# A new beginning for a two-layer hybrid decoder trunk: x in four pieces on the scalar queue, six early weight chunks, the first products by high parts, idle products between the first transposes

## The chip, the cores and the metric

The kernel runs on one core of a Trainium2 chip. The time is device time of that core in microseconds for one execution of the whole program. The core has TensorE (matrix products; PE in the rows, with PEld for the loading of its stationary operand), VectorE (DVE), ScalarE (ACT), GpSimd (POOL) and SyncE (SP), which here only issues DMAs. ScalarE can issue DMAs too; its queue is a second one beside SyncE's. Each engine works through its own instructions in order and waits on semaphores for the others.

## The reference, cut to what matters

Two layers over 256 tokens of 1024 features, all in float32:

```python
def hybrid_layer(x, ...):
    h = rms_norm(x, attn_pre_gain)
    u = h @ w_in                       # 1024 x 4120
    (qa, ka, va, qb, kcb, vcb, ksb, vsb, kwb, vwb, g_nsa, g_a, g_b) = jnp.split(u, offsets, axis=-1)
    o_a = swa_sink_attention(rope(qa), rope(ka), va, attn_sinks)
    o_b = nsa_attention(...)           # compressed, selected and window branches, gated
    mixed = sigmoid(g_a) * (o_a @ w_branch_a) + sigmoid(g_b) * (o_b @ w_branch_b)
    x = x + rms_norm(mixed @ w_out, attn_post_gain)
    h = rms_norm(x, ffn_pre_gain)
    x = x + rms_norm(conv_ffn(h, ffn_w_up, ffn_conv_w, ffn_conv_b, ffn_w_down), ffn_post_gain)
    return x
```

Only the beginning of the first layer is touched: x, its norm, and the first columns of `h @ w_in`.

## The kernel before, in words

**Split products.** A float32 product is made of three products of float32r operands. Both operands are split into a high part (rounded to float32r) and a low part (what is left): high x high, high x low and low x high are added up in PSUM (`mm3`, lines 366 to 368). For a weight chunk ScalarE writes the high part (`copy`, line 114, tile `wh`) and VectorE the low part (`sub`, line 117, tile `wl`). For x the same two engines make `xh` and `xl`; both are called `x` in the rows.

**The weight stream.** `Stream` holds all weight chunks in order of use. `load` has SyncE fetch a chunk of 512 KB into one of four staging buffers `st` (line 156); a buffer comes free when the chunk's low part has been made. `high` makes the high part and returns a function that makes the low part; `make` does both. Below, W0, W1, ... are the chunks in order: the first column tile of `w_in` (512 columns) has W0 to W3, each with 256 of the 1024 rows, the second W4 to W7, the third W8 to W11. The framework's scheduler orders each engine's instructions as they were written and as operands come free; the last argument of a chunk and `W.make` set how far ahead it is made.

**DMA lanes.** Every DMA signals on one of eight semaphores in turn, and its issue waits until the DMA eight places ahead of it has landed. So at most eight are outstanding, and an issue that waited shows when an older one landed.

**The beginning.** The tokens are two tiles of 128 (t = 0, 1). x is first loaded in three DMAs: half the features of t = 0 on ScalarE's queue (line 260), the other half, and the whole of t = 1, on SyncE's (lines 263, 265), between W0, W1 and W2. `x(t,h)` below is half h of token tile t. `first_T` transposes such a half by four transposes (line 410) and VectorE multiplies it with the gain (line 412); `first_split` has ScalarE write the high part and returns the low part. The scale of the norm itself, `rstd`, is applied later, in rope. While TensorE has nothing to do, `warm(n)` gives it n idle products of 512 columns on a tile of zeros (line 1124); `WARM` says how many stand ahead of the first transposes and how many behind them. A PSUM bank of the tag `T` (two of them) takes each group of transposes.

**The order around it.** `in_tile` runs the products of one column tile: for each chunk c and token tile t six products (two of the chunk's 128-row slices, three each). `FIRST` is the order of the pairs (t, c) in the first column tile, and `HOOKS` says which steps (further transposes, chunks to be made, `rest`) are written ahead of which pair. `rest` has ScalarE square x (line 362), GpSimd make `rstd` and its scale (lines 354, 355, 496), and VectorE, ScalarE and GpSimd the rope tables (lines 328 to 349). When a tile is done, `rope` on VectorE reads its banks, `rstd` and the tables (lines 466 to 470); `stack_T` transposes its results on TensorE (line 477) some parts later. A part is one call of `go`; `later(20, ...)` is due 20 parts on.

Of the kernel before, what the change touches and what calls it, by code (L numbers as in the profile page):

```python
# [9 lines left out]
F32 = mybir.dt.float32  # L10
# [6 lines left out]
P = 128  # L17
# [35 lines left out]
DL = {'qa0': 2, 'qa1': 13, 'ka': 6, 'qb0': 8, 'qr0': 8, 'qb1': 2, 'qr1': 4, 'cb0': 1, 'cb1': 3, 'ks': 1, 'kw': 6, 'pT': (3, 3, 2), 'pv': 4, 'hT': 1, 'ge': 3, 'pj': 4, 'cT': 5, 'cv': 9, 'yT': 1, 'h0': 5, 'h1': 4, 'uf': 0, 'x0': 3, 'x1': 3}  # L53
WARM = (6, 8)
HOOKS = {0: '1C', 1: 'B2', 2: 'D', 6: '3r'}
FIRST = [(0, 0), (0, 1), (1, 0), (1, 1), (0, 2), (1, 2), (0, 3), (1, 3)]
CMPI = (0, 0, 0, 0, 4, 6, 7, 8)
# [8 lines left out]
def tile_hybrid_trunk(  # L66
# [78 lines left out]
    class Stream:  # L145
        def __init__(self):
            self.specs, self.loaded, self.made, self.used, self.front = [], {}, {}, 0, 0

        def add(self, src, a, b, tag="w", ahead=2):
# [3 lines left out]
        def load(self, i):  # L153
            src, a, b, tag, _ = self.specs[i]
            st = wp.tile([P, a, b], F32, tag="st", bufs=4, name=nm("st"))
            nc.sync.dma_start(st, src)
            self.loaded[i] = st, a, b, tag

        def make(self, i=None):
# [99 lines left out]
    nc.sync.dma_start(cst[:, 0:P], consts[:, 0:P])  # L259
    act.dma_start(halves(X[:, 0, :])[0], halves(xv[:, 0, :])[0])  # L260
    nc.sync.dma_start(grow, attn_pre_gain[0].rearrange("(k p) -> k p", p=P))
    W.load(0)
    nc.sync.dma_start(halves(X[:, 0, :])[1], halves(xv[:, 0, :])[1])
    W.load(1)
    nc.sync.dma_start(X[:, 1, :], xv[:, 1, :])
    W.load(2)
    W.load(3)
    last_sq = [None]
# [18 lines left out]
    sink = cp.tile([P, DEPTH, 8], F32, name="sink")  # L287
    nc.sync.dma_start(sink, attn_sinks.partition_broadcast(P))
    row_load(R_B1, cmp_b1.rearrange("l k h -> (l k) h"))
    row_load(R_POS, cmp_pos_emb.rearrange("l k (pr two) d -> (l k pr) (two d)", two=2))  # L290
# [130 lines left out]
    def attn_layer(l, xp, rs, gains, first):  # L421
# [3 lines left out]
        done = set()  # L425

        def in_tile(i, tag, fin, tmajor=False, hooks={}):
            c0, w = IN_TILES[i]
# [3 lines left out]
            def go(t, c):  # L432
                if c not in chs:
                    chs[c] = W.next(2, w)
                ch = chs[c]
                tk = slice(t * P, (t + 1) * P)
                for k in range(2):
                    kk = 2 * c + k
                    o, wh, wl = bk[t][:, :w], ch[0][:, k, :], ch[1][:, k, :]
                    if i == 2:  # L440

                        o = o.rearrange("p (y x d) -> p y x d", x=2, y=2)
                        wh, wl = [v.rearrange("p (x y d) -> p y x d", x=2, y=2) for v in (wh, wl)]
                    mm3(o, xh[:, kk, tk], xl[:, kk, tk], wh, wl, kk == 0, kk == 7)
# [672 lines left out]
    def start():  # L1117
# [11 lines left out]
        dve.tensor_copy(gfirst, gb[:, 0:KD])  # L1129
        low = first_split(0, 0, first_T(0, 0), xp)  # L1130
        warm(WARM[1])
        lw = W.high(0)
        low()
        lw()

        def xs(*args):
            lows = [first_split(t, h, first_T(t, h), xp) for t, h in args]
            for f in lows:
                f()

        def rest():
            for t in range(2):
                rs[t] = rstd_of(mean_sq(halves(X[:, t, :])))
            dve.tensor_scalar(nsink, sink, -1.0, None, ALU.mult)
            rope_tables()
        act_ = {"B": lambda: xs((0, 1)), "C": lambda: xs((1, 0)), "D": lambda: xs((1, 1)), "X": lambda: xs((1, 0), (1, 1)),
                "1": lambda: W.make(1), "2": lambda: W.make(2), "3": lambda: W.make(3), "r": rest, "w": lambda: warm(3)}
        return {FIRST[i]: [act_[c] for c in h] for i, h in HOOKS.items()}

# [86 lines left out]
```

## Time and profile before

| | us |
|---|---|
| median of 3 runs | 794.11 |
| lowest and highest | 791.46, 797.75 |
| the profiled execution | 794.85 |
| its span | 793.0 |
| TensorE busy in it | 765.7 |
| VectorE, ScalarE, GpSimd busy | 613.2, 495.4, 48.1 |

The span runs from the first instruction to the last; the rest of the execution's time lies around it. In the rows, times are microseconds from the span's start. A row of the timeline is an instruction, or several alike that followed each other: start, time taken, engine, line of the kernel, operation, tile written <- tiles read (buffer numbers left out), shape, and count; in brackets how long the engine had been idle before, and what ended it. A row of a DMA queue (SPq, ACTq) is the issue of a transfer, not the transfer. A product's time in a row includes its way through the array: where products follow each other, the step from start to start is what one costs.

### The profile page before, as it was taken

The page shows a single profiled execution, that of the slowest core. Times are in us where ns is not written, and L with a number is a line of the kernel's source. Part 1 is how long each engine was busy: PE and PEld are TensorE (multiplying, and loading weights), DVE is VectorE, ACT ScalarE, POOL GpSimd, SP SyncE. Part 2 cuts the span into 40 slices and gives each one's busy share as a digit, 9 for nine tenths or more (in the row PEclk, how much of TensorE's full clock was granted, in tenths as well). Part 3 has the DMA queues.
Part 4 walks back from the last instruction along what each step waited for, and adds up shares of the span by engine and source line. Part 5 has one row for each costly group of instructions (what it writes and reads, how often), then busy time and mean ns, then how long its engine had stood idle before and what let it go on. Part 6 is the DMA issues. An engine that isn't in the chain of part 4 may idle for free.

```text
span 793.0 us, 12908 instructions
## 1 busy us (share of the span) xinstructions
PE 765.7 (97%) x4745; PEld 682.0 (86%) x4745; DVE 613.2 (77%) x1168; ACT 495.4 (62%) x948; POOL 48.1 (6%) x96
## 2 busy tenths in 40 slices
PE   8999999999899999999989999999998999999996
PEld 6689888888699999999868889888877999999995
DVE  5898888676778767777788888886867877778775
ACT  4678877744666555665555879767555655556552
POOL 2300022100100000000010000230001000000000
PEclk9999999999999999999999999999999999999999
DMA  7633156456556656666435232644645666656731
GB/s 268 218 111 123 41 160 216 144 172 205 166 168 196 187 185 183 209 218 186 157 118 173 74 121 86 206 151 135 205 137 182 193 185 186 186 184 212 216 105 53
DMA packets 42202, 131.26 MB, mean 166 GB/s; under 512 B 5359, under 2 KB 5915, under 8 KB 42139
## 3 DMA queue, kind: packets, MB, share of 16 engines
q1 hardware_dynamic: 41995, 130.18, 51.4%
q8 instruction: 37, 0.61, 0.3%
q10 hardware_dynamic: 144, 0.26, 0.1%
q14 instruction: 26, 0.21, 0.1%
HBM read 129.37 MB, written 1.05 MB: 164 GB/s over the span
## 4 chain that ended last, share of the span: by engine, by line
PE 81%; DVE 7%; ACT 7%; POOL 2%; issue 2%; DMA 1%; SPq 0%; DVEq 0%; POOLq 0%; ACTq 0%
PE mm L366 6%; PE mm L367 6%; PE mm L368 6%; PE S L367 5%; PE S L368 5%; PE S L366 5%; PE T L1000 5%; PE T L999 5%; PE mm L1000 5%; PE mm L999 5%; PE T L998 5%; PE mm L998 5%; PE O L366 3%; PE O L367 3%; PE O L368 3%; DVE wl L117 2%
## 5 line engine op out<-in xcount | busy, mean ns | idle before, releaser
L117 DVE TENSOR_TENSOR wl<-st,wh 128x1024 fp32r<-128x1024 f32 (+2 forms) x226 | 268.0, 1188 | 101.1 <-ACT wh L114 99.7
L114 ACT ACTIVATE wh<-st 128x1024 fp32r<-128x1024 f32 (+2 forms) x226 | 231.8, 1029 | 170.9 <-PE O L368 40.1
L366 PE MATMUL mm<-wh,x 128*128 128x512 f32 (+2 forms) x256 | 97.3, 382 | 0.1
L367 PE MATMUL mm<-wl,x 128*128 128x512 f32 (+2 forms) x256 | 96.2, 376 | 0.0
L368 PE MATMUL mm<-wh,x 128*128 128x512 f32 (+2 forms) x256 | 95.2, 372 | 0.0
L999 PE MATMUL mm<-q,wh 128*128 128x256 f32 x320 | 90.7, 283 | 0.0
L999 PE MATMUL T<-q,wh 128*128 128x256 f32 x320 | 90.6, 283 | 0.0
L1000 PE MATMUL T<-q,wl 128*128 128x256 f32 x320 | 90.6, 283 | 0.0
L1000 PE MATMUL mm<-q,wl 128*128 128x256 f32 x320 | 90.5, 283 | 0.0
L998 PE MATMUL T<-q,wh 128*128 128x256 f32 x320 | 90.5, 283 | 0.0
L998 PE MATMUL mm<-q,wh 128*128 128x256 f32 x320 | 90.4, 283 | 0.0
L998 PEld LDWEIGHTS mm<-q,wh 128*128 128x128 f32 x320 | 61.3, 192 | 0.9
L998 PEld LDWEIGHTS T<-q,wh 128*128 128x128 f32 x320 | 61.4, 192 | 0.8
L999 PEld LDWEIGHTS mm<-q,wh 128*128 128x128 f32 x320 | 61.3, 192 | 0.8
L999 PEld LDWEIGHTS T<-q,wh 128*128 128x128 f32 x320 | 61.4, 192 | 0.7
L1000 PEld LDWEIGHTS mm<-q,wl 128*128 128x128 f32 x320 | 61.3, 192 | 0.1
L1000 PEld LDWEIGHTS T<-q,wl 128*128 128x128 f32 x320 | 61.4, 192 | 0.0
L368 PEld LDWEIGHTS mm<-wh,x 128*128 128x128 f32 x256 | 49.2, 192 | 6.3
L366 PEld LDWEIGHTS mm<-wh,x 128*128 128x128 f32 x256 | 49.2, 193 | 5.8 <-ACT k L114 0.4
L367 PEld LDWEIGHTS mm<-wl,x 128*128 128x128 f32 x256 | 49.4, 193 | 5.6 <-DVE wl L117 0.3
L607 ACT ACTIVATE k<-k,mn 128x128 f32<-128x128 f32 (+1 forms) x96 | 42.5, 446 | 8.4 <-DVE mn L604 8.4
L354 POOL TENSOR_SCALAR rstd<-s 128x1 f32<-128x1 f32 x16 | 6.1, 381 | 520.7 <-ACT k L362 520.5
(293 smaller groups left out, 1672.9 us busy)
## 6 DMA issues: line engine op xcount, KB each, us to landing
st<-in_ffn_w_up_dram SPq DMA_DIRECT2D x88, 512.0 KB, 4.3
st<-in_w_in_dram SPq DMA_DIRECT2D x48, 512.0 KB, 3.8
st<-in_ffn_w_down_dram SPq DMA_DIRECT2D x44, 512.0 KB, 4.3
st<-in_w_out_dram SPq DMA_DIRECT2D x16, 512.0 KB, 3.6
st<-in_w_in_dram SPq DMA_DIRECT2D x16, 384.0 KB, 3.1
st<-in_cmp_w_dram SPq DMA_DIRECT2D x16, 256.0 KB, 2.6
st<-in_w_branch_a_dram SPq DMA_DIRECT2D x8, 512.0 KB, 3.6
st<-in_w_branch_b_dram SPq DMA_DIRECT2D x8, 512.0 KB, 3.6
```

Of the source, the lines that this page charges most:

```text
L114: act.activation(dst, src, AF.Copy, scale=scale)
L117: dve.tensor_tensor(dst, a, b, ALU.subtract)
L354: pool.tensor_scalar(r, s2[:, 0:1], s2[:, 1:2], EPS, ALU.add, ALU.add)
L366: pe.matmul(o, xh, wh, start=first, stop=False, skip_group_check=True)
L367: pe.matmul(o, xh, wl, start=False, stop=False, skip_group_check=True)
L368: pe.matmul(o, xl, wh, start=False, stop=last, skip_group_check=True)
L607: last_exp[0] = act.activation(self.pt[:, hh, s, :], sm[:, :nk], AF.Exp, bias=self.mn[:, i:i + 1], scale=-1.0, accum_out=self.dn[:, i:i + 1])
L998: pe.matmul(o, wh[:, k, :], hh[:, k, c0:c1], start=(k == 0), stop=False, skip_group_check=True)
L999: pe.matmul(o, wh[:, k, :], hl[:, k, c0:c1], start=False, stop=False, skip_group_check=True)
L1000: pe.matmul(o, wl[:, k, :], hh[:, k, c0:c1], start=False, stop=(k == 7), skip_group_check=True)
```

## The change

x comes in four pieces of 256 KB, all issued by ScalarE, in the order x(0,0), x(1,0), x(0,1), x(1,1). SyncE loads W0 to W3 and, behind the constants, W4 to W9 too, ahead of the small row loads. W4 to W9 don't use staging buffers: they land in three large tiles (tags `sg` and `kB`), which the attention writes much later. Both token tiles' first halves are transposed ahead of the first product, with two idle products between and three behind (`WARM`). Chunks 0 and 1 go through `products`, which for chunk 0 takes high x high of both token tiles first, then the products with the weight's low part, then those with x's. The transposes of the other halves stand behind all products of chunk 0, and the steps of the old table `HOOKS` are now written out in `start`.

```diff
-WARM = (6, 8)
-HOOKS = {0: '1C', 1: 'B2', 2: 'D', 6: '3r'}
-FIRST = [(0, 0), (0, 1), (1, 0), (1, 1), (0, 2), (1, 2), (0, 3), (1, 3)]
+WARM = (6, 2, 3)
+FIRST = [(0, 0), (1, 0), (0, 1), (1, 1), (0, 2), (1, 2), (0, 3), (1, 3)]
+EARLY = {4: ("sg", 2), 6: ("sg", 2), 8: ("kB", 1)}
...
         def load(self, i):
             src, a, b, tag, _ = self.specs[i]
-            st = wp.tile([P, a, b], F32, tag="st", bufs=4, name=nm("st"))
+            st = self.room.pop(i, None)
+            if st is None:
+                st = wp.tile([P, a, b], F32, tag="st", bufs=4, name=nm("st"))
             nc.sync.dma_start(st, src)
...
+        def early(self, i, tag, bufs):
+            both = ap_.tile([P, 2, 2, 512], F32, tag=tag, bufs=bufs, name=nm("early"))
+            self.room[i], self.room[i + 1] = both[:, 0], both[:, 1]
...
     nc.sync.dma_start(cst[:, 0:P], consts[:, 0:P])
-    act.dma_start(halves(X[:, 0, :])[0], halves(xv[:, 0, :])[0])
     nc.sync.dma_start(grow, attn_pre_gain[0].rearrange("(k p) -> k p", p=P))
-    W.load(0)
-    nc.sync.dma_start(halves(X[:, 0, :])[1], halves(xv[:, 0, :])[1])
-    W.load(1)
-    nc.sync.dma_start(X[:, 1, :], xv[:, 1, :])
-    W.load(2)
-    W.load(3)
+    for h in range(2):
+        for t in range(2):
+            act.dma_start(halves(X[:, t, :])[h], halves(xv[:, t, :])[h])
+    for i in range(4):
+        W.load(i)
...
     nc.sync.dma_start(sink, attn_sinks.partition_broadcast(P))
+    for i, (tag, bufs) in EARLY.items():
+        W.early(i, tag, bufs)
+        W.load(i)
+        W.load(i + 1)
     row_load(R_B1, cmp_b1.rearrange("l k h -> (l k) h"))
...
+        def products(t, c, bk, chs, w):
+            todo = [(tt, p, k) for p in ((0, 0), (0, 1), (1, 0)) for tt in range(2) for k in range(2)] if c == 0 else \
+                   [(t, p, k) for p in ((0, 0), (1, 0), (0, 1)) for k in range(2)]
+            if c == 0:
+                todo = todo[6 * t:6 * t + 6]
+            for tt, (xp_, wp_), k in todo:
+                tk = slice(tt * P, (tt + 1) * P)
+                pe.matmul(bk[tt][:, :w], (xh, xl)[xp_][:, 2 * c + k, tk], chs[c][wp_][:, k, :],
+                          start=(c == k == xp_ == wp_ == 0), stop=False, skip_group_check=True)
...
+                if first and i == 0 and c < 2:
+                    products(t, c, bk, chs, w)
+                    return
...
-        low = first_split(0, 0, first_T(0, 0), xp)
+        m0 = first_T(0, 0)
+        lw0 = W.high(0)
+        low0 = first_split(0, 0, m0, xp)
         warm(WARM[1])
-        lw = W.high(0)
-        low()
-        lw()
-
-        def xs(*args):
-            lows = [first_split(t, h, first_T(t, h), xp) for t, h in args]
+        low1 = first_split(1, 0, first_T(1, 0), xp)
+        warm(WARM[2])
+        lw0()
+        low0()
+        low1()
+        W.make(1)
+
+        def second():
+            m0, m1 = first_T(0, 1), first_T(1, 1)
+            lw = W.high(2)
+            lows = [first_split(t, 1, m, xp) for t, m in ((0, m0), (1, m1))]
+            lw()
             for f in lows:
                 f()
...
+        steps = {2: [second], 4: [lambda: W.make(3)], 5: [rest]}
+        return {FIRST[i]: fns for i, fns in steps.items()}
```

TensorE's first instructions before: `S` is the bank of the idle products, `T` a bank of transposes, `mm_159` the bank of token tile 0 and `wh_154`, `wl_155` the two parts of W0; `x_8` holds the high parts of x, `x_9` the low ones.

```order
L1124 MATMUL S_128<-k_61_126 128x512 x6
L1128 MATMUL T_135<-cst,k_2_76 128x8
L410 MATMUL T_138<-cst,X 128x128 x4
L1124 MATMUL S_128<-k_61_126 128x512 x8
L410 MATMUL T_165<-cst,X 128x128 x4
L366 MATMUL mm_159<-wh_154,x_8_108 128x512
L367 MATMUL mm_159<-wl_155,x_8_108 128x512
L368 MATMUL mm_159<-wh_154,x_9_109 128x512
```

And now: `mm_179` and `mm_180` are the banks of token tiles 0 and 1, `wh_155` and `wl_156` the parts of W0, `x_11` the high and `x_12` the low parts of x.

```order
L1148 MATMUL S_138<-k_64_136 128x512 x6
L1152 MATMUL T_145<-cst,k_2_76 128x8
L420 MATMUL T_148<-cst,X 128x128 x4
L1148 MATMUL S_138<-k_64_136 128x512 x2
L420 MATMUL T_161<-cst,X 128x128 x4
L1148 MATMUL S_138<-k_64_136 128x512 x3
L445 MATMUL mm_179<-wh_155,x_11_118 128x512 x2
L445 MATMUL mm_180<-wh_155,x_11_118 128x512 x2
L445 MATMUL mm_179<-wl_156,x_11_118 128x512 x2
L445 MATMUL mm_180<-wl_156,x_11_118 128x512 x2
L445 MATMUL mm_179<-wh_155,x_12_119 128x512 x2
L445 MATMUL mm_180<-wh_155,x_12_119 128x512 x2
```

The second group of transposes, of the other token tile, moved in among the idle products, and the low parts of W0 and x are asked for four and eight products later.

VectorE before, from the last step of the rope table on: `wl_322`, `wl_346`, `wl_352` are the low parts of W4, W5 and W6, and lines 466 and 468 are rope on the first column tile.

```order
L342 TENSOR_SCALAR k_89_253<-k_89_253 128x64
L117 TENSOR_TENSOR wl_322<-st_319,wh_321 128x1024
L466 SCALAR_TENSOR_TENSOR k_90_280<-mm_159,rstd_240,tab 128x512
L468 SCALAR_TENSOR_TENSOR k_91_281<-mm_159,rstd_240,tab 128x8x32 x2
L117 TENSOR_TENSOR wl_346<-st_343,wh_345 128x1024
L470 TENSOR_TENSOR k_90_280<-k_90_280,k_91_281 128x512
L117 TENSOR_TENSOR wl_352<-st_349,wh_351 128x1024
```

And now, from the middle of the table steps: `wl_327`, `wl_349`, `wl_353`, `wl_357` are the low parts of W4 to W7, `wl_373` and `wl_389` those of W8 and W9, and lines 490 and 492 are rope.

```order
L349 SCALAR_TENSOR_TENSOR k_92_254<-k_92_254 128x64 x3
L117 TENSOR_TENSOR wl_327<-early_98,wh_326 128x1024
L350 TENSOR_SCALAR k_92_254<-k_92_254 128x64
L117 TENSOR_TENSOR wl_349<-early_98,wh_348 128x1024
L351 SCALAR_TENSOR_TENSOR k_92_254<-k_92_254 128x64
L117 TENSOR_TENSOR wl_353<-early_101,wh_352 128x1024
L352 TENSOR_SCALAR k_92_254<-k_92_254 128x64
L117 TENSOR_TENSOR wl_357<-early_101,wh_356 128x1024
L490 SCALAR_TENSOR_TENSOR k_93_287<-mm_179,rstd_241,tab 128x512
L492 SCALAR_TENSOR_TENSOR k_94_288<-mm_179,rstd_241,tab 128x8x32 x2
L117 TENSOR_TENSOR wl_373<-early_104,wh_372 128x1024
L494 TENSOR_TENSOR k_93_287<-k_93_287,k_94_288 128x512
```

All four low parts of the second column tile now stand ahead of rope on the first one, where only that of W4 did. From the middle of the fourth column tile on, the order of each engine is the one before the change.

## Rows read from the trace of the kernel before

**Rows 1.** The page: busy time and share of the span of each engine.
```profile
PE 765.7 (97%) x4745; PEld 682.0 (86%) x4745; DVE 613.2 (77%) x1168; ACT 495.4 (62%) x948; POOL 48.1 (6%) x96
```
**Rows 2.** Busy times by stretches: stretch, length, busy by engine, granted clock, DMA.
```profile
0.00:20.00 20.00, 16.68 (x66) 12.98 (x67) 10.58 (x15) 8.54 (x13) 4.84 (x10) 1.00 0.74 266
20.00:40.00 20.00, 18.11 (x82) 14.04 (x81) 17.52 (x38) 13.22 (x24) 5.95 (x14) 1.00 0.65 216
40.00:60.00 20.00, 18.75 (x117) 16.20 (x116) 18.59 (x69) 15.99 (x46) 0.00 (x0) 0.92 0.34 109
```
**Rows 3.** Timeline of TensorE: the fill, and the first column tile's first and last products.
```profile
1.44 2.93 PE L1124 MATMUL S<-k 128*128 128x512 f32 x6 [1.44 <-DVE k L1119]
...
5.06 1.11 PE L410 MATMUL T<-cst,X 128*128 128x128 f32 x4
5.83 3.58 PE L1124 MATMUL S<-k 128*128 128x512 f32 x8
10.77 0.63 PE L410 MATMUL T<-cst,X 128*128 128x128 f32 x4 [1.36 <-DMA X<-in_x_dram]
11.16 0.48 PE L366 MATMUL mm<-wh,x 128*128 128x512 f32 x1
...
22.86 0.39 PE L367 MATMUL mm<-wl,x 128*128 128x512 f32 x1
23.09 0.39 PE L368 MATMUL mm<-wh,x 128*128 128x512 f32 x1
```
**Rows 4.** Timeline of SyncE's queue: issues that waited until an older transfer had landed.
```profile
6.65 0.43 SPq L288 DMA_DIRECT2D sink<-in_attn_sinks_dram  x1
8.06 0.27 SPq L281 DMA_DIRECT2D k<-in_cmp_b_dram  x1
...
10.65 0.34 SPq L281 DMA_DIRECT2D k<-in_ffn_conv_w_dram  x1
...
13.29 0.29 SPq L281 DMA_DIRECT2D k<-in_ffn_conv_w_dram  x1
```
**Rows 5.** Timeline of VectorE and ScalarE: the steps that make x and W ready.
```profile
6.21 0.69 DVE L412 TENSOR_TENSOR k<-T,gfirst 128x512 f32<-128x512 f32 x1 [0.88 <-PE T L410]
6.93 0.63 ACT L114 ACTIVATE x<-k 128x512 fp32r<-128x512 f32 x1 [4.27 <-DVE k L412]
...
9.38 1.06 ACT L114 ACTIVATE wh<-st 128x1024 fp32r<-128x1024 f32 x1 [0.87 <-DMA st<-in_w_in_dram]
10.47 1.23 DVE L117 TENSOR_TENSOR wl<-st,wh 128x1024 fp32r<-128x1024 f32 x1 [0.70 <-ACT wh L114]
```
**Rows 6.** Timeline of TensorE and VectorE: the waits in the second column tile.
```profile
24.38 0.50 PE L367 MATMUL S<-wl,x 128*128 128x512 f32 x1 [0.45 <-DVE wl L117]
26.15 0.75 DVE L466 SCALAR_TENSOR_TENSOR k<-mm,rstd,tab 128x512 f32<-128x512 f32 x1 [1.82 <-POOL tab L348]
28.88 0.50 PE L367 MATMUL S<-wl,x 128*128 128x512 f32 x1 [1.44 <-DVE wl L117]
```
**Rows 7.** Timeline of ScalarE: the first of four squares of x.
```profile
19.29 0.61 ACT L362 ACTIVATE k<-X 128x512 f32<-128x512 f32 x1
```
**Rows 8.** Timeline of GpSimd and VectorE: a scale made alone, and beside a low part.
```profile
21.75 0.30 POOL L496 TENSOR_SCALAR rq<-rstd 128x1 f32<-128x1 f32 x1
23.11 1.22 DVE L117 TENSOR_TENSOR wl<-st,wh 128x1024 fp32r<-128x1024 f32 x1
23.23 1.20 POOL L496 TENSOR_SCALAR rq<-rstd 128x1 f32<-128x1 f32 x1
```
**Rows 9.** Timeline of TensorE, and stretches as in rows 2, behind 56 us.
```profile
56.34 0.53 PE L477 MATMUL T<-ident_r,k 128*128 128x128 f32 x4 [1.08 <-ACT q L114]
56.00:57.00 1.00, 0.66 (x6) 0.66 (x7) 0.61 (x6) 1.00 (x4) 0.00 (x0) 0.93 0.00 0
57.00:58.00 1.00, 1.00 (x6) 0.99 (x6) 0.89 (x5) 1.00 (x4) 0.00 (x0) 0.50 0.00 0
...
60.00:61.00 1.00, 1.00 (x9) 1.00 (x8) 1.00 (x7) 1.00 (x5) 0.00 (x0) 0.86 0.00 0
```

More of the change, by code (lines that the diff above doesn't have):

```diff
@@ L147, in __init__ @@
             self.specs, self.loaded, self.made, self.used, self.front = [], {}, {}, 0, 0
+            self.room = {}
         def add(self, src, a, b, tag="w", ahead=2):
@@ L1145, in rest @@
             rope_tables()
-        act_ = {"B": lambda: xs((0, 1)), "C": lambda: xs((1, 0)), "D": lambda: xs((1, 1)), "X": lambda: xs((1, 0), (1, 1)),
-                "1": lambda: W.make(1), "2": lambda: W.make(2), "3": lambda: W.make(3), "r": rest, "w": lambda: warm(3)}
-        return {FIRST[i]: [act_[c] for c in h] for i, h in HOOKS.items()}
+        steps = {2: [second], 4: [lambda: W.make(3)], 5: [rest]}
+        return {FIRST[i]: fns for i, fns in steps.items()}
     more_rows()
```

## The prediction

> **What bounds the kernel now.** I read the busy shares first. TensorE is busy for 97% of the span [rows 1], so the time is its work plus the stretches in which it has nothing to do. The table by stretches of 20 us says where those lie: 3.3 us in the first stretch, 1.9 in the second, 1.25 in the third [rows 2]. Behind the third stretch the order of every engine is the one before the change, so 6.5 us of idle time, and what the first products lose by their place and their clock, is all that the change can reach.
>
> Then the timeline of TensorE in the first stretch. It fills with idle products (six, then eight), transposes the first piece of x, and its first real product starts at 11.16 us; just ahead of it stands a wait of 1.36 us, which a DMA of X ends [rows 3]. That DMA is the whole second token tile, 512 KB. SyncE's next issues tell when transfers have landed, since each waits for an older one: W0 was in by 6.65, x(0,1) by 8.06, X of the second token tile by 10.65, W3 by 13.29 [rows 4]. From 8.06 to 13.29 four transfers of 512 KB landed, 0.40 MB per us; the queues are full there, and nothing can be had but a better order.
>
> Last the waits in the second column tile: TensorE stands 0.45 us before 24.38 and 1.44 before 28.88, both for a low part made by VectorE. VectorE was not too slow there: it waited 1.82 us for the rope table from GpSimd, and in its order rope stands ahead of the low part of W5 [rows 6].
>
> **Term 1: the first column tile.** x(1,0) must land first. x(0,0) is there by 5.06, when its transposes start. x(1,0) follows it alone on the scalar queue, against W0 on the other. At half of 0.40 MB/us its 0.26 MB take 1.3 us, at a third 2.0: 6.4 or 7.0. In the profile x(0,1) needed 1.41 us behind W0 with no second queue beside it [rows 4], twice the full rate; with that x(1,0) comes at 8.06. TensorE is through its two idle products at 5.83 + 2 x 0.45 = 6.73, so earlier does not help. I take 7.2, bounds 6.73 and 8.06.
>
> From there, with the durations of [rows 3, 5]: transposes 1.11 (first group at 5.06) to 8.31; product with the gain 0.69 to 9.0; x high part 0.63 to 9.65. ScalarE has done W0's high part (1.06 from 6.65) and x(0,0)'s (0.63) by 8.35. TensorE has its three idle products after 0.77 for issuing the transposes: 7.2 + 0.77 + 3 x 0.45 = 9.3, and starts its first products there, 1.9 us sooner than before. VectorE makes W0's low part (1.23) by 10.25 and x's two low parts (taken as 0.69 each, the same size) by 10.95 and 11.65. With the high products first, four products need no low part, four need W0's, two the part of 10.95 and the last two that of 11.65; at 0.23 us each (the step from 22.86 to 23.09) [rows 3] they follow those times almost without a hole and end at 12.1. Two groups of transposes take 0.39 each (10.77 to 11.16): 12.9. The 36 products left need 35 x 0.23 to the start of the last: 20.95, where it was 23.09. The cover holds: VectorE goes on with W1's low part (12.9), two products with the gain (14.3), W2's low part (15.5), two x low parts (16.9) and W3's (18.1), which chunks 2 and 3, from 15.65 and 18.4 on, ask for at about those times. **-2.15 us**; with the bounds of x(1,0) -2.6 to -1.3.
>
> Three idle products fewer cost nothing by themselves, for TensorE waited behind them anyway. But they hold the clock. The eight took 3.58 us, 0.45 each: 512 columns at the 1.2 GHz level, though the profile's row grants full speed from the start; 0.23 is the 2.4 GHz level. Before, the fill had run to 9.41, and the products at 11.16 ran at 2.4. Now the fill has a hole, and products start at 9.3. Each product at the low level costs 0.22 more; none of the first twelve, or all, is 0 to +2.6. I take two or three: **+0.5**.
>
> **Term 2: six early chunks.** W4 to W9 no longer wait for one of the four staging buffers. They queue behind W3 (13.29) and 0.3 MB of constants: at 0.40 MB/us W4 is in by about 15.4 and W9 by 22. ScalarE comes to W4 after W3 (about 16) and four squares of 0.61 [rows 7]: about 18.5 to 19.5. VectorE's order now has W4's low part inside the table steps, and W5 to W7 ahead of rope; each takes 1.23, so they end near 21, 22.3, 23.6 and 24.9. TensorE wants them at 21.2, then every 12 x 0.23 = 2.8 us. Both waits go: **-1.9** (0.45 + 1.44), bounds 0 and -1.9. What is late next is rope and the low parts of W8 and W9, wanted only after a further tile of 48 x 0.23 = 11 us.
>
> The six loads also pass the small row loads on SyncE's queue, some 8 us of transfer. Their reader is due 20 parts in, in the middle of the third column tile; that cover is wide. Four issues in place of one on ScalarE push the table load back, hidden because ScalarE's first operand is W0, 6.65. W2's load now waits for x(0,0): hidden, the queues hold 1.5 MB then. All zero.
>
> **Term 3: after 50 us.** TensorE waits 1.08 before 56.34 for a copy on ScalarE, and runs at the low level after it [rows 9]. In the new order one of the query copies stands ahead of the exponentials. I take half of the wait: **-0.5**, bounds 0 and -1.08.
>
> **Term 4: given back.** VectorE is 88% and 93% busy in the second and third stretch [rows 2]; it can't come forward by all of this. **+0.4**, bounds 0 and +1.9 (all of term 2).
>
> **Sum**: -2.15 + 0.5 - 1.9 - 0.5 + 0.4 = -3.65. The profiled execution took 794.85: 791.2. It lay 0.74 above the median of the runs shown, so against 794.11 it is 790.5.
>
> **Rivals.**
> x comes late: x(1,0) at 8.06 (+0.9) and with it two more products at the low level (+0.4). For it speaks the slow x(0,1); against it, that x has a queue of its own. 791.8.
>
> VectorE becomes the bound. GpSimd's 128x1 step at 23.23 took 1.20 us, where the like of it took 0.3, and ended just behind VectorE's low part of 23.11 to 24.33 [rows 8]. Four low parts now stand where GpSimd makes the scales and tables; the eight table steps may end some 2 us later, rope with them, and then W8's low part. Against it: VectorE would idle at rope, leaving GpSimd free, and TensorE wants W8 only at about 32. If it bites, term 2 is lost: 792.4. The Trainium skill, SBUF — State Buffer, section SBUF: two separate sides, speaks against the change here: a VectorE operation with two SBUF inputs and a GpSimd operation that reads SBUF share one port pair as an exclusive lock, and the second blocks for the whole instruction. By that rule, the trace agrees: 1.20 us against 0.30; the time by it is this rival's.
>
> The clock holds after 56 us. The low stretch lasts from 56 to 61 with granted shares 0.93, three times 0.50, 0.86 [rows 9]: 1.7 us of full speed lost. If the shorter wait keeps the level up, 788.8.
>
> Slower: the level does not rise. If the holed fill leaves TensorE at 1.2 GHz, each product costs 0.22 more; after 17 such beyond those counted the gain is gone, which is when the low level lasts to about 18 us. With 30 in all it ends at 796.6. Against it: from 9.3 on TensorE is never without work, and before it was at 2.4 by 11.16 in spite of 1.36 us without any.
>
> **How the numbers follow.** Forecast 0.48, x late 0.18, VectorE 0.13, clock held 0.13, level low 0.08. The likeliest, 790.5, is the number; its own range is 788.5 to 792. The range from 787.0 to 794.5 takes in the late x, VectorE and the held clock, with a us on each side since the three runs shown lie 6 us apart; it leaves out the low level. 1%, about what a measurement of this kernel can tell from no change, is 7.9 us. Faster than that needs the held clock and every term at its bound: 0.03. Slower needs more than 50 products at the low level: 0.02. Within: 0.95.
>
> **What would show it.** First product at about 9.3, with pairs of one weight part; last product of the first tile near 21; no wait of TensorE for a low part from 21 to 32; the 1.08 wait shorter. The steps of the first products (0.45 or 0.23) show the level. Wrong would be: a wait for X beyond 8.1, idle time for low parts in the third tile, or a low stretch after 12 us.

## The result, and the profile after

The changed kernel takes 788.71 us in the median (786.59 to 791.11, 7 runs), where the kernel before takes 794.11 (791.46 to 797.75, 7 runs beside it). The ratio is 0.9931, with a 95% interval from 0.9908 to 0.9954: 0.7% less, which is within the 1% that the forecast called no change, and 1.8 us under the 790.5 that it gave. The profiled execution of after took 788.22 us, 6.63 less than that of before; its span is 786.4.

The page of after, busy time and share of the span by engine; it answers to [rows 1]:

```profile
PE 759.8 (97%) x4742; PEld 676.1 (86%) x4742; DVE 612.5 (78%) x1168; ACT 494.7 (63%) x948; POOL 51.2 (7%) x96
```

The same three stretches of 20 us as in [rows 2]:

```profile
0.00:20.00 20.00, 17.41 (x77) 13.56 (x78) 14.81 (x27) 13.33 (x22) 8.71 (x16) 1.00 0.90 338
20.00:40.00 20.00, 19.01 (x96) 15.37 (x94) 17.22 (x34) 10.70 (x19) 5.17 (x9) 1.00 0.59 199
40.00:60.00 20.00, 19.54 (x138) 17.17 (x137) 18.77 (x70) 18.36 (x55) 0.00 (x0) 1.00 0.17 54
```

TensorE is busy for 0.7, 0.9 and 0.8 us more in them than before, and it has more to show for it: 77, 96 and 138 instructions in place of 66, 82 and 117. ScalarE and VectorE have moved forward in the first stretch (13.33 us of work in place of 8.54, and 14.81 in place of 10.58), and the transfers moved 338 GB/s there in place of 266.

The timeline of TensorE, from the idle products ahead of the transposes of x(1,0) to the first product of the fifth column tile (start, length, idle time ahead in brackets):

```profile
5.05 0.71 PE L1148 MATMUL S<-k 128*128 128x512 f32 x2
5.60 0.60 PE L420 MATMUL T<-cst,X 128*128 128x128 f32 x4
5.95 0.95 PE L1148 MATMUL S<-k 128*128 128x512 f32 x3
7.91 1.25 PE L445 MATMUL mm<-wh,x 128*128 128x512 f32 x4 [1.01 <-ACT x L114]
...
10.82 1.04 PE L420 MATMUL T<-cst,X 128*128 128x128 f32 x8
...
19.68 0.39 PE L378 MATMUL mm<-wh,x 128*128 128x512 f32 x1
...
29.44 0.51 PE L501 MATMUL T<-ident_r,k 128*128 128x128 f32 x4 [0.99 <-DVE k L117]
...
32.16 0.39 PE L378 MATMUL S<-wh,x 128*128 128x512 f32 x1
...
48.40 0.45 PE L378 MATMUL mm<-wh,x 128*128 128x512 f32 x1
...
64.37 0.40 PE L376 MATMUL mm<-wh,x 128*128 128x512 f32 x1
```

ScalarE takes in W0 and then makes the high parts of x ahead of that first product (timeline of ScalarE of after):

```profile
6.28 1.06 ACT L114 ACTIVATE wh<-st 128x1024 fp32r<-128x1024 f32 x1 [2.17 <-DMA st<-in_w_in_dram]
7.24 1.13 ACT L114 ACTIVATE x<-k 128x512 fp32r<-128x512 f32 x2
```

The first product starts at 7.91 (before 11.16), the last one of the first column tile at 19.68 (23.09) [rows 3]. The waits of 0.45 and 1.44 us for low parts [rows 6] are gone, the wait of 1.08 us behind 56 us [rows 9] too; a new one of 0.99 us stands ahead of four transposes at 29.44. For the other three places the timeline of TensorE of before has these rows:

```profile
37.29 0.39 PE L368 MATMUL S<-wh,x 128*128 128x512 f32 x1
...
52.73 0.39 PE L368 MATMUL mm<-wh,x 128*128 128x512 f32 x1
...
70.41 0.39 PE L366 MATMUL mm<-wh,x 128*128 128x512 f32 x1
```

So after is ahead by 3.41 us at the end of the first tile, 5.13 at the end of the second, 4.33 at the end of the third, and 6.04 when the fifth starts. That the third tile seems to give 0.8 back is a matter of where the transposes stand: counted from a tile's first product to the first of the next tile, TensorE has 54 instructions in the second tile where it had 58, and 114 in the third where it had 106. The two together gained 0.92.

Behind that the two traces run side by side, product for product, 5.9 us apart, up to 370 us, and what then moves them is not the change. Two stretches of before have the low level where after has none (stretch, length, busy by engine, granted clock, DMA; of before):

```profile
402.00:404.00 2.00, 2.00 (x7) 1.62 (x7) 1.49 (x3) 0.60 (x1) 1.30 (x3) 0.50 0.49 154
...
446.00:448.00 2.00, 2.00 (x12) 2.00 (x11) 2.00 (x9) 2.00 (x8) 0.00 (x0) 0.50 0.00 0
```

Between the same products, the lead grows by 1.24 us over the first and 1.26 over the second. And after loses 1.73 around 508 us, where a weight chunk came late and ScalarE and then TensorE waited for it (timelines of ScalarE and TensorE of after):

```profile
506.24 1.06 ACT L114 ACTIVATE wh<-st 128x1024 fp32r<-128x1024 f32 x1 [1.22 <-DMA st<-in_w_in_dram]
...
508.10 0.75 PE L619 MATMUL S<-kB,q 128*128 128x256 f32 x4 [1.56 <-ACT k L114]
```

5.9 + 1.24 + 1.26 - 1.73 is 6.67, and the last products lie 6.68 apart. The start of the fifth tile is therefore the better measure of a part of the change: times of one kernel lie up to 6 us apart, while this place repeats to 0.4 us in three profiles of the changed kernel (64.37, 64.77, 64.52), and nearly all of the 0.4 lies in the first tile: from its end to the fifth tile the three take 44.69, 44.77 and 44.70.

### The profile page after: what moved, and what is told of

It is laid out like the page before. It is cut to its first block, busy times and chain, and to the rows that moved or that the text cites. A ratio compares the mean times of both kernels' runs of the same rounds, so it can differ in the third digit from the quotient of the medians.

```text
span 786.4 us, 12903 instructions
## 1 busy us (share of the span) xinstructions
PE 759.8 (97%) x4742; PEld 676.1 (86%) x4742; DVE 612.5 (78%) x1168; ACT 494.7 (63%) x948; POOL 51.2 (7%) x96
## 4 chain that ended last, share of the span: by engine, by line
PE 80%; ACT 7%; DVE 6%; POOL 3%; issue 2%; DMA 1%; DVEq 0%; SPq 0%; POOLq 0%; ACTq 0%
PE mm L376 6%; PE mm L377 6%; PE mm L378 6%; PE T L1024 5%; PE T L1023 5%; PE mm L1024 5%; PE mm L1023 5%; PE T L1022 5%; PE mm L1022 5%; PE S L377 5%; PE S L378 5%; PE S L376 5%; PE O L376 3%; PE O L377 3%; PE O L378 3%; DVE wl L117 2%
## 5 line engine op out<-in xcount | busy, mean ns | idle before, releaser
L117 DVE TENSOR_TENSOR wl<-st,wh 128x1024 fp32r<-128x1024 f32 (+2 forms) x220 | 260.6, 1186 | 102.5 <-ACT wh L114 101.2
L114 ACT ACTIVATE wh<-st 128x1024 fp32r<-128x1024 f32 (+2 forms) x220 | 225.8, 1029 | 174.8 <-PE O L378 41.5
L376 PE MATMUL mm<-wh,x 128*128 128x512 f32 (+2 forms) x248 | 92.5, 375 | 0.1
L377 PE MATMUL mm<-wl,x 128*128 128x512 f32 (+2 forms) x248 | 91.7, 370 | 0.1
L378 PE MATMUL mm<-wh,x 128*128 128x512 f32 (+2 forms) x248 | 91.1, 368 | 0.1
L378 PEld LDWEIGHTS mm<-wh,x 128*128 128x128 f32 x248 | 46.6, 188 | 6.3 <-DVE x L117 0.5
L377 PEld LDWEIGHTS mm<-wl,x 128*128 128x128 f32 x248 | 46.7, 188 | 5.2 <-DVE wl L117 0.3
L376 PEld LDWEIGHTS mm<-wh,x 128*128 128x128 f32 x248 | 46.5, 188 | 5.4 <-ACT k L114 0.4
```

What stands on the lines that cost most here:

```text
L114: act.activation(dst, src, AF.Copy, scale=scale)
L117: dve.tensor_tensor(dst, a, b, ALU.subtract)
L376: pe.matmul(o, xh, wh, start=first, stop=False, skip_group_check=True)
L377: pe.matmul(o, xh, wl, start=False, stop=False, skip_group_check=True)
L378: pe.matmul(o, xl, wh, start=False, stop=last, skip_group_check=True)
```

## The experiments

Twelve more runs followed, of nine new kernels (z3 repeats y1) and, twice, of the changed one. The table gives for each the start of the first product, of the last product of the first, second and third column tile, and of the first product of the fifth (all from the timeline of TensorE), the time from the end of the third to the fifth, and the times: the median and its ratio to the kernel before on the same chip.

| run | first | tile 1 | tile 2 | tile 3 | fifth | 3 to 5 | median, us | ratio (95%) |
|---|---|---|---|---|---|---|---|---|
| before | 11.16 | 23.09 | 37.29 | 52.73 | 70.41 | 17.68 | 794.11 | |
| after | 7.91 | 19.68 | 32.16 | 48.40 | 64.37 | 15.97 | 788.71 | 0.9931 (0.9908 to 0.9954) |
| x1: after, no early chunks | 8.11 | 19.90 | 33.34 | 50.05 | 65.99 | 15.94 | 790.65 | 0.9969 (0.9958 to 0.9980) |
| x2: before, early chunks | 11.28 | 24.08 | 37.78 | 53.56 | 69.94 | 16.38 | 793.58 | 1.0003 (0.9989 to 1.0017) |
| x3: after, x on SyncE's queue | 9.18 | 20.96 | 33.97 | 49.65 | 67.11 | 17.46 | 793.25 | 0.9996 (0.9983 to 1.0009) |
| x4: after, usual product order | 7.80 | 20.41 | 32.85 | 49.14 | 65.11 | 15.97 | 789.83 | 0.9949 (0.9932 to 0.9967) |
| y1: after, tables on ScalarE | 7.92 | 20.06 | 31.43 | 47.62 | 63.58 | 15.96 | 788.16 | 0.9934 (0.9915 to 0.9952) |
| y2: after, no late fill | 7.98 | 21.36 | 33.83 | 50.07 | 66.03 | 15.96 | 791.08 | 0.9972 (0.9958 to 0.9986) |
| y3: after, W0 ahead of the gain | 10.82 | 23.13 | 35.63 | 51.88 | 67.87 | 15.99 | 791.70 | 0.9981 (0.9964 to 0.9998) |
| y4: after again | 8.06 | 20.00 | 32.50 | 48.80 | 64.77 | 15.97 | 788.03 | 0.9931 (0.9909 to 0.9954) |
| z1: before, new x loads | 8.65 | 22.55 | 36.31 | 52.10 | 68.47 | 16.37 | 792.94 | 0.9986 (0.9973 to 0.9999) |
| z2: x1 with low parts ahead of rope | 8.10 | 19.85 | 33.13 | 49.34 | 65.31 | 15.97 | 789.92 | 0.9945 (0.9927 to 0.9963) |
| z3: y1 again | 7.91 | 19.70 | 31.08 | 47.30 | 63.28 | 15.98 | 787.56 | 0.9914 (0.9897 to 0.9931) |
| z4: after again | 8.01 | 19.82 | 32.30 | 48.55 | 64.52 | 15.97 | 789.63 | 0.9937 (0.9920 to 0.9954) |

**The early chunks taken out, and put in alone.** x1 empties the table:

```
-EARLY = {4: ("sg", 2), 6: ("sg", 2), 8: ("kB", 1)}
+EARLY = {}
```

> The changed kernel with its table of six early chunks emptied: W4 to W9 come through the four staging buffers again, and behind the row loads. Theory (term 2): the first column tile stays as in the changed kernel, last product at 19.7 us, but VectorE's order puts rope ahead of the low part of W5 again, TensorE waits about 1.5 us in the second tile, so its last product starts near 33.7 instead of 32.16, and the fifth tile starts at 66 to 67 instead of 64.37; time about 790.5. Rival (the chunks were in time anyway, the gain of the second tile comes from the earlier first tile alone): 32.2 and 64.4, time 788.7.

x2 adds the table, `early` and the six loads behind `sink` to the kernel before, and nothing else.

> The kernel before with the six early chunks alone, its beginning and its x loads as before. Theory A (what frees the second tile is that the chunks are there): first tile as before, last product at 23.1, second tile 35.4 instead of 37.29, fifth tile starts at 68.5 instead of 70.41; time about 792.2. Theory B (what frees it is where VectorE's order puts the low parts against rope; here the low part of W5 still stands behind rope): 37.3 and 70.4, time 794.

The timelines of ScalarE, VectorE and TensorE of x1, and then of TensorE of x2:

```profile
19.18 2.94 ACT L114 ACTIVATE wh<-st 128x1024 fp32r<-128x1024 f32 x3
21.73 0.75 DVE L490 SCALAR_TENSOR_TENSOR k<-mm,rstd,tab 128x512 f32<-128x512 f32 x1 [1.62 <-POOL tab L358]
23.19 1.22 DVE L117 TENSOR_TENSOR wl<-st,wh 128x1024 fp32r<-128x1024 f32 x1
...
24.46 0.50 PE L377 MATMUL S<-wl,x 128*128 128x512 f32 x1 [1.20 <-DVE wl L117]
...
48.91 0.54 PE L501 MATMUL T<-ident_r,k 128*128 128x128 f32 x4 [0.80 <-ACT q L114]
```
```profile
10.53 1.09 PE L422 MATMUL T<-cst,X 128*128 128x128 f32 x4 [2.45 <-DMA X<-in_x_dram]
...
25.25 0.50 PE L379 MATMUL S<-wl,x 128*128 128x512 f32 x1 [0.33 <-DVE wl L118]
...
29.75 0.50 PE L379 MATMUL S<-wl,x 128*128 128x512 f32 x1 [1.47 <-DVE wl L118]
```

Taken out of the changed kernel, they cost 1.62 us at the fifth tile (65.99 against 64.37; 1.2 to 1.6 against the three profiles of the changed kernel) and about 2 in the median. The wait for W5's low part comes back with 1.20, and a wait of 0.80 for a query copy appears in the third tile; on the other hand x1, whose rope starts at 21.73, has no wait like the 0.99 at 29.44 of after. Put alone into the kernel before, they bring nothing: ScalarE waits for none of the six chunks, and both waits stand as they did, 0.33 and 1.47. (That the first tile of x2 ends 0.99 later has another reason: behind its hole of 2.45 us the first products ran at the low level.) In both kernels VectorE's order has rope ahead of the low part of W5. The rows of x1 show that W5 itself was there in time: ScalarE made the high parts of W5, W6 and W7 from 19.18 on, VectorE the low part of W5 only at 23.19, behind the first steps of rope. So this wait is not one for a load; it comes from the place that the scheduler gives the low part in VectorE's order. That the whole gain of the early chunks comes from such places is theory B of x2.

z2 asks for that place without the loads: x1, with the low parts of W5 and W6 made and rope held behind them.

```
 def fin_a(t, b):
+    if first and t == 0:
+        while W.front < 7:
+            W.make()
+    with behind(W.low_ins[6] if first and t == 0 else None):
         q_rot(qA, t, 0, heads(b, 0, 8), ...)
```

> The changed kernel without early chunks (W4 to W9 through the four staging buffers, behind the row loads), but with the low parts of W5 and W6 ahead of rope in VectorE's order, as the early chunks had put them. Theory (the order on VectorE gives the gain of the second tile, not the earlier loads): the wait of 1.20 us at 24.46 of the run without early chunks is gone, second tile's last product 32.2 to 32.5 with a first tile that ends near 19.8, time 788.9 to 789.7. Rival (the loads are needed): W5 or W6 is not there, TensorE waits about 1 us or more in the second tile all the same, last product 33 or later, time 790.6.

The waits of TensorE in the second tile of z2:

```profile
21.47 0.50 PE L378 MATMUL S<-wl,x 128*128 128x512 f32 x1 [0.53 <-DVE wl L117]
...
29.76 0.51 PE L502 MATMUL T<-ident_r,k 128*128 128x128 f32 x4 [0.72 <-DVE k L117]
```

The wait of 1.20 is gone, as the order wants it; but the second tile ends at 33.13, neither where the theory put it nor much better than x1. In this kernel ScalarE makes all the high parts of the second tile behind the two sines, W4's at 19.12 where x1 has it at 16.95, so W4's low part is late by 0.53 instead. At the fifth tile z2 stands between the two, 65.31. The order on VectorE gives 0.7 of the 1.6 us, in one profile each. Most of the rest went to the other order on ScalarE, which came with this form of the test, so the theory is only half shown.

**x on one queue.** x3 puts the four pieces on SyncE's queue, in the order of need:

```
 for h in range(2):
     for t in range(2):
-        act.dma_start(halves(X[:, t, :])[h], halves(xv[:, t, :])[h])
-for i in range(4):
-    W.load(i)
+        nc.sync.dma_start(halves(X[:, t, :])[h], halves(xv[:, t, :])[h])
+    W.load(2 * h)
+    W.load(2 * h + 1)
```

> The changed kernel with the four pieces of x on SyncE's queue too, in the order x(0,0), x(1,0), W0, W1, x(0,1), x(1,1), W2, W3. Theory A (the order of the bytes is all; one queue fills the transfer engines as well as two): x(1,0) lands near 4.9, W0 near 6.3, first product near 7.9, last product of the first tile 19.7, time 788.7. Theory B (a second queue brings throughput: 338 GB/s over the first 20 us in place of 266): W0 lands 1 us later, first product near 9, first tile's last product 20.7 or later, fifth tile's start 65.4 or later, time 789.7 or more.

SyncE's queue, then ScalarE and TensorE, of x3:

```profile
1.57 0.83 SPq L271 DMA_DIRECT2D X<-in_x_dram  x2
2.44 0.91 SPq L159 DMA_DIRECT2D st<-in_w_in_dram  x2
...
7.55 1.06 ACT L114 ACTIVATE wh<-st 128x1024 fp32r<-128x1024 f32 x1 [5.33 <-DMA st<-in_w_in_dram]
...
9.18 1.26 PE L445 MATMUL mm<-wh,x 128*128 128x512 f32 x4 [1.74 <-ACT x L114]
...
53.26 0.54 PE L501 MATMUL T<-ident_r,k 128*128 128x128 f32 x4 [1.22 <-ACT q L114]
```

The times of theory B hold, its reason only in part. W0 is there 1.27 us later (7.55 against the 6.28 at which ScalarE takes it in after), the first product 1.27, the tile 1.28. The rows say how: two issues of x, 0.83 us together, stand ahead of W0's, which starts at 2.44 in place of 1.58. From 7 to 13 us both kernels move the same, 363 and 367 GB/s; before 7 us it is 185 against 242. Where the queues are full the second one doesn't make the transfers faster; it lets them begin sooner. The Trainium skill says this much in DMA: Bandwidth & Descriptors, section Issuing engines are not separate DMA queues: issuing from several engines saves only the sequencer's time to initiate, usually small beside the transfer. The trace agrees in so far as the rates from 7 to 13 us are the same; here the 0.86 us of issuing saved went with 1.27 us at W0's landing and 1.28 at the end of the tile, and where the other 0.4 come from the rows do not say. The rest of the 2.74 us that x3 loses at the fifth tile comes behind the third tile, and is taken up with the clock below.

**The order of the first products.** x4 gives chunks 0 and 1 the usual order (`if first and i == 0 and c < 2` becomes `if False`).

> The changed kernel with the products of chunks 0 and 1 in the usual order, high by high, high by low, low by high for each half of a chunk, in place of all high products first. Theory A (it is worth what term 1 says): TensorE starts at 7.9 but waits for W0's low part (8.6) and x's low parts (9.2, 9.9), chunk 0 ends about 0.7 us later, last product of the first tile 20.4, time 789.4. Theory B (VectorE's low parts of W2 and W3 set the end of the tile, so the order at its start is hidden): 19.7, time 788.7.

```profile
8.54 0.49 PE L377 MATMUL mm<-wl,x 128*128 128x512 f32 x1 [0.24 <-DVE wl L117]
```

That row of x4's TensorE is the wait for W0's low part that theory A names, and the tile ends at its 20.4: 20.41, 0.73 later than after, and 0.74 at the fifth tile. The other two profiles of the changed kernel end the tile at 20.00 and 19.82; from the first product to the last it takes 11.77 to 11.94 us in the three, and 12.61 here. So the order is worth some 0.7 to 0.8, and VectorE's later low parts do not hide it.

**The fill.** y2 takes the five late idle products out: `WARM = (6, 0, 0)`.

> The changed kernel without the five idle products between and behind the first transposes (six, none, none). Theory A (the clock stays up after the first six): nothing changes, since TensorE waits there for ScalarE anyway; first product 7.9, last product of the first tile 19.7, time 788.7. Theory B (the hole of some 2.8 us ahead of 7.9 lets the level fall, as the hole of 2.45 us did in the kernel before with early chunks, low from 10.24 to 13.65): a low stretch of 3.41 us lies over the first products, which costs about 1.7 us: last product 21.4, fifth tile's start 66, time 790.4.

TensorE of y2, and a stretch with the granted clock (the last number but two):

```profile
7.98 1.74 PE L445 MATMUL mm<-wh,x 128*128 128x512 f32 x4 [2.11 <-ACT x L114]
9.52 1.91 PE L445 MATMUL mm<-wl,x 128*128 128x512 f32 x4
...
9.00:10.00 1.00, 1.00 (x4) 0.71 (x3) 0.91 (x3) 0.93 (x1) 0.00 (x0) 0.50 1.03 422
```

Theory B holds, and its 1.7 us too (21.36 against 19.68). The first product starts when it did. But after 2.11 us without work the level falls to 1.2 GHz under the first products: the first four take 1.74 where after needs 1.25, the next four 1.91. The five idle products, in a time in which TensorE has nothing else to do, are worth 1.7 us in the trace (1.4 against y4), and 3.0 in the median against y4, which was timed beside it.

**W0 ahead of the gain.** y3 issues W0's load ahead of the 4 KB load of the gain, to have W0's landing, which sets 7.91, a little sooner.

```
-nc.sync.dma_start(grow, attn_pre_gain[0]...)
 ...
+W.load(0)
+nc.sync.dma_start(grow, attn_pre_gain[0]...)
-for i in range(4):
+for i in range(1, 4):
     W.load(i)
```

> The changed kernel with W0's load ahead of the small load of the gain on SyncE's queue, 0.4 us sooner. Theory (W0's landing at 6.26, then its high part, set the first product at 7.91): W0's high part starts 0.4 us sooner, first product at 7.5, last product of the first tile 19.3 instead of 19.68, fifth tile 64.0. Rival (VectorE's low parts or later chunks set the tile): first product 7.5, but last product still 19.6 to 19.7.

Neither came, since W0 did not land sooner. SyncE's queue, ScalarE and TensorE of y3:

```profile
1.17 0.42 SPq L159 DMA_DIRECT2D st<-in_w_in_dram  x1
1.63 0.38 SPq L272 DMA_DIRECT2D k<-in_attn_pre_gain_dram  x1
...
6.30 1.06 ACT L114 ACTIVATE wh<-st 128x1024 fp32r<-128x1024 f32 x1 [2.19 <-DMA st<-in_w_in_dram]
...
6.74 0.24 PE L1153 MATMUL T<-cst,k 8*128 8x8 f32 x1 [2.37 <-DMA k<-in_attn_pre_gain_dram]
```

W0 was issued 0.41 us sooner and landed no sooner (6.30 against 6.28). The gain was issued 0.46 later, and its transpose starts 2.23 later, at 6.74 in place of 4.51; everything on TensorE waits behind it, the first four products (from 10.82 on, some 0.43 us each) are still at the low level, and the first tile ends at 23.13. Here the 4 KB load arrived only when the 512 KB ahead of it on the same queue had. So whether W0's landing sets the first product is not answered by y3; x3 speaks for it, where both came 1.27 later.

**The x loads alone.** z1 is the kernel before with the new loads of x, all else kept.

> The kernel before with the new loads of x alone (four pieces on the scalar queue, W0 to W3 behind the gain on SyncE's), its fill of six and eight, its order of the first products and no early chunks. Theory (the late landing of the second token tile was what held the first tile): no wait for X is left, first product when the fill of eight is through, at 8.4 to 9.8 by the level, last product of the first tile about 21.2 instead of 23.09, the waits of the second tile stay (1.9 us), fifth tile's start about 68.5 instead of 70.41, time about 792. Rival (VectorE, which makes each piece of x alone in this order and waits 0.7 us for ScalarE in each, is the bound): last product at 22.5 or later, time within 0.7 of the kernel before.

VectorE and TensorE of z1:

```profile
7.04 0.69 DVE L117 TENSOR_TENSOR x<-k,x 128x512 fp32r<-128x512 f32 x1 [0.70 <-ACT x L114]
...
16.66 0.50 PE L365 MATMUL mm<-wl,x 128*128 128x512 f32 x1 [0.60 <-DVE wl L117]
...
55.69 0.54 PE L475 MATMUL T<-ident_r,k 128*128 128x128 f32 x4 [1.08 <-ACT q L114]
...
57.00:58.00 1.00, 1.00 (x11) 1.00 (x10) 1.00 (x4) 1.00 (x5) 0.00 (x0) 1.00 0.00 0
```

The rival has it: the first product is 2.5 us sooner (8.65), but the tile ends at 22.55, 0.54 sooner. In this order VectorE multiplies a piece by the gain, waits 0.70 us until ScalarE has its high part, and makes the low part, four times one after the other; the changed kernel does two pieces at a time, which leaves no wait of that kind. Early data were worth little until the order of their users had changed. The time, 792.94, is 1.28 below the 794.22 of the kernel before timed beside it, more than the 0.7 that the rival allowed. The fifth tile's start, 68.47, is what the theory gave, but by luck: 1.3 of the 1.94 us gained there are the low stretch that this profile does not have (last row).

**The tables on ScalarE.** The new wait of 0.99 us at 29.44 has a chain behind it (VectorE and GpSimd of after):

```profile
20.47 3.39 POOL L359 TENSOR_SCALAR tab<-k 128x64 f32<-128x64 f32 x4
...
21.75 1.21 DVE L117 TENSOR_TENSOR wl<-early,wh 128x1024 fp32r<-128x1024 f32 x1
23.82 1.35 POOL L358 TENSOR_SCALAR tab<-k 128x64 f32<-128x64 f32 x4
24.55 0.75 DVE L490 SCALAR_TENSOR_TENSOR k<-mm,rstd,tab 128x512 f32<-128x512 f32 x1 [1.59 <-POOL tab L358]
```

Four table steps beside VectorE's low parts take 0.85 us each, the four behind them, while VectorE mostly waits, 0.34; rope waits 1.59 us for them, and the transposes of its result stand in the second tile. y1 makes the eight steps on ScalarE (`copy(tab[...], c, f)` in place of `pool.tensor_scalar`), and z3 is the same kernel once more.

> The changed kernel with the eight steps that scale the rope tables on ScalarE instead of GpSimd; the order of every other instruction stays. Theory (GpSimd's table steps are blocked beside VectorE's low parts, four of them took 3.39 us, so rope starts late at 24.55 and TensorE waits 0.99 us before 29.44): the eight steps take about 2 us on ScalarE, which has a gap there, rope starts near 23.2, the wait at 29.44 is gone, second tile's last product 31.2 instead of 32.16, fifth tile's start 63.4 instead of 64.37, time about 787.7. Rival (VectorE's own load is the bound, the table only fills its idle time): rope earlier, the wait stays within 0.3 of 0.99, fifth tile 64.4, time 788.7.

> The kernel with the rope tables scaled on ScalarE once more, timed in more rounds beside the changed kernel. If it beats the changed kernel by what the start of the fifth tile says (0.8 to 1.2 us), its median lies at 787.5 to 787.9 against 788.3 to 788.7, a ratio to the kernel before lower by 0.0010 to 0.0015; if what is won is given back behind the fifth tile, the two ratios agree.

ScalarE and VectorE of z3:

```profile
22.12 1.28 ACT L114 ACTIVATE tab<-k 128x64 f32<-128x64 f32 x8
...
22.85 0.74 DVE L490 SCALAR_TENSOR_TENSOR k<-mm,rstd,tab 128x512 f32<-128x512 f32 x1
```

All eight take 1.28 us, rope starts 1.7 us sooner and without a wait, and TensorE no longer waits in the second tile, which takes 11.37 and 11.38 us in place of 12.48 to 12.50. Both times the fifth tile starts 1.2 us sooner than in the changed kernel timed beside it (63.58 against 64.77, 63.28 against 64.52). That is the theory. The times bear it out only in part, since a us is less than they scatter: 788.16 against 788.03 in y1, 787.56 against 789.63 in z3. By the trace this version is faster than both kernels; by the times it is faster than the kernel before, and not shown to be faster than after.

**The changed kernel again.** y4 and z4 repeat it.

> The changed kernel once more, unchanged. If the low stretches at 401 and 446 us in the profile of before were chance of that execution and not of the kernel, some executions of the changed kernel have them too, and this profile or its neighbours show a lower mean clock at times up to 791. The first 70 us should come out the same: first product at 7.9 to 8.2, fifth tile's start 64.2 to 64.8, with no low stretch at 50 to 55 since no wait stands there; the ratio to the kernel before 0.992 to 0.995.

> The changed kernel for comparison in the same call: ratio to the kernel before 0.992 to 0.9945, median 788 to 789.

The beginning repeats to 0.4 us. The low stretches near 400 and 445 us come and go from execution to execution: y4 has one of them (granted clock, a stretch of y4), z4 both, and of the fourteen profiles only that of after has neither. So the 2.5 us that they make between the two profiles compared above are chance, and the rarer case is the one of after.

```profile
397.00:398.00 1.00, 1.00 (x3) 0.79 (x3) 0.82 (x3) 0.20 (x1) 0.88 (x3) 0.50 0.45 168
```

## Why the prediction was right, and where its steps were not

The time was right, and so was the sign of every term but the clock's, which was nothing; the sum of the steps up to the fifth tile was -3.65 and came out as -4.7, or -6.04 with a low stretch that is no fixed part of the change. That the time fell where it did is in part a balance of errors: term 1 with its clock gave 1.8 us more than forecast, terms 2 and 4 gave 0.6 less. And that the median lies within 0.1 of the rival's 788.8 is chance, for the steps without that low stretch come out 1.1 us beyond the forecast already.

**Term 1** (-2.15, and +0.5 for the clock) measured -3.41. The step that failed is the landing of x(1,0). It was taken at 7.2, with 6.73 as the earliest; its transposes ran at 5.60, straight behind the two idle products and without a wait. In z2 they started at 5.42, again without a wait, so there x(1,0) had landed by then. The rate had been read from x(0,1) of before [rows 4], which came behind W0 on one queue; x3 shows that a queue of its own for x lets W0 come sooner as well. "Earlier does not help" was wrong too: TensorE was through its two idle products at 5.60 (in y4 at 6.26), not at 6.73. With x out of the way the first product was set by what the prediction had done by 8.35 and hidden, ScalarE's high parts behind W0's landing, and started at 7.91 instead of 9.3. From there the working held: the last product of the tile was to start 11.65 us behind the first, and did so after 11.77. The cost of the clock was 0 here. In this profile the fill behind the first six already ran at the full level, which is chance: in y4 the two idle products between the transposes took 1.20 us together in place of 0.71, and there too the first product came at 8.06, no product of the first tile was at the low level, and the tile ended 0.3 later. That the question was the right one is shown by y2, where the low level cost 1.7.

What the term did not say is that the loads are worth little without the new order. Put alone into the kernel before, they are worth 0.54 (z1); taken out of the changed kernel, the order of products is worth 0.73 (x4), the second queue 1.28 (x3), the late fill 1.68 (y2). From z1's 22.55 to x1's 19.90 lie 2.65 us, of which x4 explains some 0.7; what the rest owes to taking x two pieces at a time, to the order of the pairs and to the shorter fill, no run separates.

**Terms 2 and 4** (-1.9 and +0.4) measured -0.92 together. The low parts of W4 to W7 came where the order put them, 1.8 to 1.9 us ahead of the times given since the tile before them was ahead, and both waits went. What was mis-sized is what is given back: 0.99 in one new wait. It is the mechanism of the rival in which VectorE and GpSimd block each other, with another victim: rope is late, as the rival says, but what TensorE then waits for is not the low part of W8; it is the operand of the transposes at 29.44, the result of rope, which the prediction did not look at. By the rule of the Trainium skill, SBUF — State Buffer, section SBUF: two separate sides, GpSimd blocks for a whole instruction of VectorE that has two SBUF inputs. The trace agrees, 0.85 against 0.34 us a step, and y1 and z3 give its price here, 1.2 us and not the 1.9 of the rival. The prediction also credited the early loads; x1, x2 and z2 say that VectorE's order is at least a good part of it, and how much of the rest is the loads' own stays open.

**Term 3** (-0.5 of 1.08) measured -0.40. The last column but two of the table shows it: from the end of the third tile to the fifth it takes 15.94 to 15.99 us in ten profiles, 16.37 and 16.38 in the two that have the wait of 1.08 us and no low stretch behind it (z1, x2), and 17.68 and 17.46 in the two that have the wait and the low stretch (before, x3). So the wait costs 0.40 net, and the low stretch behind it 1.1 to 1.3. The reason given, the place of one query copy, is borne out. Behind the exponentials ScalarE has two query copies in the four profiles with that wait, and one or none in the ten others; of before, and then of after:

```profile
55.72 1.05 ACT L114 ACTIVATE q<-T 128x512 fp32r<-128x512 f32 x2
```
```profile
51.47 0.57 ACT L114 ACTIVATE q<-T 128x512 fp32r<-128x512 f32 x1
```

**The clock behind 56 us**, a rival with 0.13, is what happened in the two profiles compared. It was priced with 1.7 us and is worth 1.3. None of the ten profiles without the wait has a low stretch there, two of the four with it do; whether the change takes it away for good or only makes it rarer, fourteen profiles do not settle.

**The other rivals.** x did not come late, and no run shows what that would have cost; what x3 delays is W0. The level did not fail to rise, but y2 shows what stood between: without its late fill the kernel would have lost 1.7 of what it gained.

## What to carry to other kernels

Loads that come earlier help only as far as the order of the engines that use them lets them: look at which instruction stands ahead of the user in its own engine's order before counting on a transfer. Fill a hole of about 2 us on TensorE ahead of its first real work with idle products, and issue small loads that gate the start, such as a gain of 4 KB, ahead of every large one on their queue. Measure a change of a few us at a place in the trace that repeats, not by the whole time alone.

## What the runs showed of the hardware

The granted clock falls in some executions and not in others at the same place in the program: at about 400 and 445 us in z4, at one of the two in y4, at neither in the profile of after, three executions of one kernel. A hole of 2.11 us (y2) or 2.45 us (x2) ahead of the first products was followed by the low level both times; holes of 1.36 (before), 1.38 (z2) and 1.74 us (x3) there were not. In x2 the low level lay over the first products:

```profile
11.00:12.00 1.00, 1.00 (x5) 0.90 (x5) 0.81 (x2) 0.00 (x0) 0.00 (x0) 0.50 0.58 194
```
